# The last norm of a two-layer trunk: 1/rms of the last columns by logarithm and Exp, and one operation for weight and 1/rms

## The chip, the cores and the metric

The kernel runs on one core of a Trainium2 chip. Such a core has engines that run side by side, each with a queue of its own: TensorE (PE in the profile) multiplies matrices, VectorE (DVE) and ScalarE (ACT) work element by element, GpSimd (POOL) and SyncE (SP) here mostly issue transfers. An engine takes its queue in order and waits at an instruction until what it needs is there. Transfers between the chip's memory and the core's own memory (DMA) are issued from the queues of SP, ACT and POOL and run on 16 shared DMA engines. The metric is device time in microseconds, from the start of the program to its end; less is better.

## The reference

The reference is a decoder trunk for one sequence of 1024 positions with 1024 features: a short-convolution layer and a dilated-attention layer, each followed by a SwiGLU feed-forward block, and a norm at the very end. Only the end matters here:

```
def rms_norm(x, g):
    xf = x.astype(jnp.float32)
    y = xf * lax.rsqrt(jnp.mean(xf * xf, axis=-1, keepdims=True) + EPS)
    return (y * g.astype(jnp.float32)).astype(x.dtype)
...
        h = rms_norm(x, ffn_norm[i])
        x = x + swiglu(h, ffn_w_gate[i], ffn_w_up[i], ffn_w_down[i])
    return rms_norm(x, final_norm)
```

So every output element is x times 1/rms, which belongs to its position, times a weight (the gain), which belongs to its feature. The 1/rms of a position needs the squares of all its 1024 features, and these are complete only when the last product has been added to x.

## The kernel before

The residual x lies in eight tiles `X[n]`, n = 0 to 7, each of 128 partitions (features) and 1024 columns (positions). A gain is therefore one number per partition, and 1/rms is one number per column, the same in all partitions. A sum over features is a sum over partitions and over the eight tiles; TensorE makes it with a matrix of ones, which also puts the result into every partition.

A product in nearly full precision is made of three fast ones: each operand is split into a high part and a low remainder (`split`, lines 134 to 146: a copy on ScalarE at L144, a subtraction on VectorE at L145), and high by high, high by low and low by high are added up (lines 372 to 374). A product of two plain float32 operands is also possible; TensorE then runs it as two half-products.

The last feed-forward block ends with products that are done by columns (`by_columns`). The 1024 columns are cut into three pieces: 0 to 511, 512 to 767 and 768 to 1023. For each piece, and in it for each of the eight tiles n, TensorE makes twelve products (four tiles of the inner dimension, three parts each) into one of its eight accumulation banks; then `add_to_x` (L491, VectorE) adds the bank to x. In the first piece the weights are loaded and split as well, three tiles ahead. After each tile `each` and `between` (through `tile_done`), inside `final`, add their work to the queues:

- `each`: ScalarE squares the new columns of x (L1930 for tile 0, straight into the running sum `acc`; L1933 for the others, into a page `sq`). Then ScalarE multiplies the columns of x by the gain, in place (L1935).
- `between(i, n)`: VectorE adds the squares of the tile before to `acc` (`add_squares`, L1940), one tile behind so that it needn't wait for ScalarE. Then come the steps of the norm of the piece before, i - 1: at n = 1 its sum of squares is split (L144, L145); at n = 3 `spread_sums` multiplies both parts by ones (L485), and ScalarE makes 1/rms as Exp of -1/2 times the logarithm (L486, L487). At the same n = 3 the eight scalings of that piece are put into a list. Then one scaling is taken from the list (`some(1)`).
- `scaled`: one scaling, VectorE multiplies the columns of a tile by 1/rms (L1944), and the result is sent out (L1945), from SP's queue for even tiles and from ACT's queue for odd ones.

The order is written out by hand: each engine's queue holds its instructions in the order in which this code issues them. A scaling in `between` stands on VectorE ahead of the next tile's addition, and a transfer on ACT's queue stands ahead of the next square.

For the last piece there are no further tiles to do its norm beside, and it has a way of its own. `squared_sum` multiplies `acc` and the last tile's squares, 128 columns at a time, by one column of ones (L1958, L1960), which gives two columns with one sum per partition. ScalarE takes the square root, VectorE the reciprocal (L1963); VectorE makes from it and the identity matrix `eye` two diagonal matrices side by side (L1965), and `spread` multiplies these by ones (L1973), which brings 1/rms back into every partition. Between `squared_sum` and `spread` stand the scalings of the piece before that are left in the list. The root needs another function table on ScalarE than logarithm and Exp; it is loaded in piece 2 at n = 3 (L1990). The identity is loaded at the start, from POOL's queue (L1885).

Of the kernel before, what the change touches and what calls it, by code (L numbers as in the profile page):

```python
# [10 lines left out]
F32 = mybir.dt.float32  # L11
F32R = mybir.dt.float32r
AF = mybir.ActivationFunctionType
ALU = mybir.AluOpType
# [4 lines left out]
D = 1024  # L19
DF = 2816  # L20
H = 16
KT = D // 128
# [72 lines left out]
def view(t, off, dims):  # L95
    return bass.AP(tensor=t.tensor, offset=t.offset + off, ap=[t.ap[0]] + [list(d) for d in dims])
# [3 lines left out]
def trunk(ctx: ExitStack, tc: tile.TileContext, x, gains_in, cwi, ck, cwo, wqkv, wo, relb,  # L100
          wg, wu, wd, oneh, ident, out):
    nc = tc.nc
    consts = ctx.enter_context(tc.tile_pool(name="consts", bufs=1))
# [5 lines left out]
    def page(name, dt=F32):  # L109
        return pages.tile([128, 1024], dt, name=name, tag="page", bufs=PAGES)  # L110
# [3 lines left out]
    def half_page(name, dt=F32):  # L114
        return scope["pool"].tile([128, 512], dt, name=name, tag="half", bufs=scope["halves"])

    def bank():
        return psum.tile([128, 512], F32, name="bank", tag="bank")
# [7 lines left out]
    taps = consts.tile([128, KT, 3], F32)  # L126
    ones = consts.tile([128, 128], F32)
    ones_r = consts.tile([128, 128], F32R)
    eye = consts.tile([128, 128], F32)
    eps = consts.tile([128, 1], F32)  # L130
    scratch = consts.tile([128, 1], F32)
    zcol = consts.tile([128, 2, 1], F32)
# [32 lines left out]
    def ensure(upto):  # L165
        while op_state[0] < min(upto + 1, len(ops)):
            key = ops[op_state[0] + 1][0] if op_state[0] + 1 < len(ops) else None
            if key in sums_of:
                sums_of.pop(key)()
            made[op_state[0]] = ops[op_state[0]][1]()  # L170
            op_state[0] += 1

    def take(key, ahead=1):
        i = op_state[1]
        assert ops[i][0] == key, (ops[i][0], key)
        ensure(i + ahead)
        op_state[1] += 1
        return made.pop(i)
# [198 lines left out]
    def run(*gens):  # L377
        for _ in zip(*gens):
            pass
        for g in gens:  # L380
            for _ in g:
                pass
# [12 lines left out]
    X = [None] * KT  # L395
# [86 lines left out]
    def spread_sums(rstd, sums):  # L482
        b = bank()[:, :rstd.shape[1]]
        for i, t in enumerate(sums):
            nc.tensor.matmul(b, ones_r, t, start=i == 0, stop=i == len(sums) - 1)  # L485
        nc.scalar.activation(rstd, b, AF.Ln, scale=1.0 / D, bias=eps)  # L486
        nc.scalar.activation(rstd, rstd, AF.Exp, scale=-0.5)  # L487

    def add_to_x(n, banks):
        for (c0, c1), b in banks.items():  # L490
            nc.vector.tensor_tensor(out=X[n][:, c0:c1], in0=X[n][:, c0:c1], in1=b[:, :c1 - c0], op=ALU.add)  # L491
# [749 lines left out]
    class Swiglu(Strassen):  # L1241
# [111 lines left out]
        def feed_forward(self, stats, last_step, after, final=None):  # L1353
# [27 lines left out]
            if final:  # L1381
                final(key, self.plain, self.hid)
                return
# [4 lines left out]
    def by_columns(key, ks, acts, pieces, each, between, wide=4, ahead=1, added=lambda i, n: None):  # L1388

        w = {}  # L1390
        for i, piece in enumerate(pieces):
            for n in range(KT):
                if i == n == 0:
                    w.update({m: take(key + (m,)) for m in range(wide)})
                    ensure(op_state[1] + ahead)
                    banks = {m: {piece: bank()} for m in range(wide)}
                    run(*[product(w[m], ks, acts, banks[m]) for m in banks])
                elif i or n >= wide:
                    if i == 0:
                        w[n] = take(key + (n,), min(ahead, KT - 1 - n) or 1)  # L1400
                    banks = {n: {piece: bank()}}
                    run(product(w[n], ks, acts, banks[n]))
                add_to_x(n, banks[n])
                added(i, n)
                each(n, piece)
                between(i, n)
# [475 lines left out]

    load_first()
    nc.gpsimd.dma_start(taps, ck)
    nc.gpsimd.dma_start(eye, ident)  # L1885
    nc.vector.memset(ones, 1.0)
    nc.vector.memset(ones_r.bitcast(F32), 1.0)
    nc.vector.memset(eps, EPS)
# [6 lines left out]
    with tc.tile_pool(name="first", bufs=1) as scope["pool"]:  # L1895
# [4 lines left out]
        norm = Norm(1)  # L1900
# [13 lines left out]
    with tc.tile_pool(name="third", bufs=1) as scope["pool"]:  # L1914
        scope["halves"] = 20
        sw, group1, *rest = into_ffn(1, Norm(3))
        group1("ao", range(AO, 8), acts)
        norm = Norm(4)

        def final(key, ks, hid):  # L1920
            pieces = ((0, HALF), (HALF, 768), (768, S))
            sums, scale = [], []

            def each(n, c):

                s = slice(*c)
                if norm.acc is None:
                    norm.acc, norm.rstd = page("acc"), page("rstd")
                if n == 0:
                    nc.scalar.activation(norm.acc[:, s], X[n][:, s], AF.Square)  # L1930
                else:
                    sq = page("sq")
                    nc.scalar.activation(sq[:, s], X[n][:, s], AF.Square)  # L1933
                    sums.append((sq, s))
                nc.scalar.activation(X[n][:, s], X[n][:, s], AF.Identity, scale=norm.gain(n))  # L1935

            def add_squares(keep=0):
                while len(sums) > keep:
                    sq, s = sums.pop(0)
                    nc.vector.tensor_tensor(out=norm.acc[:, s], in0=norm.acc[:, s], in1=sq[:, s], op=ALU.add)  # L1940

            def scaled(i, n, rstd):
                s = slice(*pieces[i])
                nc.vector.tensor_tensor(out=X[n][:, s], in0=X[n][:, s], in1=rstd, op=ALU.mult)  # L1944
                (nc.sync, nc.scalar)[n % 2].dma_start(out[n][:, s], X[n][:, s])  # L1945

            def some(k):
                for _ in range(min(k, len(scale))):
                    scaled(*scale.pop(0))

            def squared_sum(i, extra=None):

                c0, c1 = pieces[i]
                nt = (c1 - c0) // 128
                b = bank()
                for t in range(nt):
                    cols = slice(c0 + 128 * t, c0 + 128 * t + 128)
                    nc.tensor.matmul(b[:, t:t + 1], norm.acc[:, cols], ones[:, 0:1], start=True, stop=extra is None)  # L1958
                    if extra is not None:
                        nc.tensor.matmul(b[:, t:t + 1], extra[:, cols], ones[:, 0:1], start=False, stop=True)  # L1960
                r = consts.tile([128, KT], F32, name="r", tag="r", bufs=2)
                nc.scalar.activation(r[:, :nt], b[:, :nt], AF.Sqrt, scale=1.0 / D, bias=eps)
                nc.vector.reciprocal(r[:, :nt], r[:, :nt])  # L1963
                diag = half_page("diag")
                nc.vector.tensor_tensor(out=view(diag, 0, [[128, nt], [1, 128]]),  # L1965
                                        in0=view(eye, 0, [[0, nt], [1, 128]]),
                                        in1=view(r, 0, [[1, nt], [0, 128]]), op=ALU.mult)
                return diag[:, :c1 - c0]

            def spread(diag):  # L1970
                b = bank()
                w = diag.shape[1]
                nc.tensor.matmul(b[:, :w], ones, diag, start=True, stop=True)  # L1973
                return b[:, :w]

            known = []

            def between(i, n):
                add_squares(int(n > 0))
                if (i, n) == (0, 5):  # L1980
                    nc.scalar.preload_act_table_set(LN_EXP)
                if i and n == 1:
                    s = slice(*pieces[i - 1])
                    known.append(split(norm.acc[:, s], [half_page("sum", F32R)[:, :s.stop - s.start] for _ in range(2)]))
                elif i and n == 3:
                    s = slice(*pieces[i - 1])
                    spread_sums(norm.rstd[:, s], known.pop())
                    scale.extend((i - 1, k, norm.rstd[:, s]) for k in range(KT))
                    if i == len(pieces) - 1:
                        nc.scalar.preload_act_table(AF.Sqrt)  # L1990
                some(1)

            def tile_done(i, n):
                if i < len(pieces) - 1 or n < KT - 1:
                    between(i, n)

            by_columns(key, ks, hid, pieces, each, tile_done, 1, 3)
            last = len(pieces) - 1
            add_squares(1)
            diag = squared_sum(last, sums.pop()[0])  # L2000
            some(KT)
            rstd = spread(diag)
            for n in range(KT):
                scaled(last, n, rstd)

        sw.feed_forward(*rest, None, final)


# [48 lines left out]
```

## Time and profile before

| what | value |
|---|---|
| median of three runs | 2113.32 us (2112.34 to 2113.49) |
| profiled execution | 2113.6 us |
| its span in the trace | 2111.8 us |
| TensorE busy | 2088.2 us, 99% of the span |
| VectorE busy | 1737.2 us, 82% |
| ScalarE busy | 1021.1 us, 48% |
| last product of the last block ends | 2100.1 us |
| last scaling ends | 2108.3 us |

The profile is one execution, recorded by the chip; its times are counted from the start of the span. In a row of the timeline stand the start, the duration, the engine, the line of the kernel, the operation, what is written from what, the shape, the count, and in brackets how long the engine had been idle and what ended that. A row with a count above one merges neighbours: its duration runs from the start of the first to the end of the last. Two instructions of one engine can overlap by a little, so the distance between two starts is often less than a duration. The rows of the windows give for a stretch of time its length, then the busy time of TensorE, of its weight loads, of VectorE, ScalarE and GpSimd, then the clock granted to TensorE (1.00 is full speed), the mean busy share of the DMA engines and the GB/s that they moved. The rows of groups give the busy time of all instructions of a kind and the mean in ns of one.

### The profile page before, as it was taken

To read this page: it belongs to the slowest core of one execution; us is meant where nothing else is said; L and a number is where in the kernel's file an instruction comes from. 1 tells how busy PE (TensorE), PEld (TensorE's weight loads), DVE (VectorE), ACT (ScalarE), POOL (GpSimd) and SP (SyncE) were. 2 spreads that over 40 slices of the span, in tenths; PEclk is the share of its full clock that TensorE was granted. 3 is DMA by queue.
4 is the path that set the end of the run, shared out by engine and by line. 5 is a ranking of instruction groups with operands and counts; after the bars stand their busy time and mean duration, and the time that the engine had idled before them with its cause. 6 is when DMAs were issued, how large, how long until landed. Compare 5 with 4: busy or idle time off the path is not lost. (4 is left out here: it accounts for less than half of the span.)

```text
span 2111.8 us, 30764 instructions
## 1 busy us (share of the span) xinstructions
PE 2088.2 (99%) x11006; PEld 1796.4 (85%) x11006; DVE 1737.2 (82%) x3255; ACT 1021.1 (48%) x1868; POOL 236.8 (11%) x337
## 2 busy tenths in 40 slices
PE   9999999999999999999999999999999999999998
PEld 7788888888888888887799999988788888888887
DVE  8898769988888888968967687987998888888876
ACT  7433427443434554446545555555544434456435
POOL 1000000110101000010322222211011011001000
PEclk9999999999999999999999999999999999999999
DMA  7322643323333476351767777955223333358432
GB/s 221 95 95 70 229 135 75 105 100 110 115 100 107 155 206 203 121 157 65 244 210 190 170 184 191 250 190 140 70 90 105 105 106 105 115 187 244 158 95 80
DMA packets 141527, 300.77 MB, mean 142 GB/s; under 512 B 48252, under 2 KB 54478, under 8 KB 141376
## 3 DMA queue, kind: packets, MB, share of 16 engines
q1 hardware_dynamic: 107488, 201.94, 32.7%
q0 software_dynamic: 26256, 82.18, 12.3%
q10 hardware_dynamic: 7632, 14.70, 1.8%
q8 instruction: 87, 1.43, 0.3%
q14 instruction: 64, 0.52, 0.1%
HBM read 208.49 MB, written 82.93 MB: 138 GB/s over the span
## 5 line engine op out<-in xcount | busy, mean ns | idle before, releaser
L572 PE MATMUL bank<-b,w 128*128 128x512 f32 x1952 | 761.3, 390 | 5.1 <-DVE w L145 4.9
L570 PE MATMUL bank<-b,w 128*128 128x512 f32 x1952 | 761.7, 390 | 3.6 <-ACT w L144 2.3
L571 PE MATMUL bank<-b,w 128*128 128x512 f32 x1952 | 761.2, 390 | 0.6 <-DVE b L881 0.6
L572 PEld LDWEIGHTS bank<-b,w 128*128 128x128 f32 x1952 | 366.9, 188 | 85.6 <-DVE w L145 9.4
L570 PEld LDWEIGHTS bank<-b,w 128*128 128x128 f32 x1952 | 367.0, 188 | 80.1 <-ACT w L144 3.1
L571 PEld LDWEIGHTS bank<-b,w 128*128 128x128 f32 x1952 | 367.1, 188 | 75.6 <-DVE b L881 1.5
L144 ACT ACTIVATE w<-combo 128x512 fp32r<-128x512 f32 (+2 forms) x488 | 249.2, 540 | 237.8 <-DVE combo L192 220.6
L145 DVE TENSOR_TENSOR w<-combo,w 128x512 fp32r<-128x512 f32 (+2 forms) x488 | 276.5, 580 | 37.9 <-ACT w L144 37.1
L576 ACT ACTIVATE part<-bank 128x512 f32<-128x512 f32 x186 | 110.7, 595 | 377.7 <-PE bank L572 377.4
L145 DVE TENSOR_TENSOR w<-raw,w 128x512 fp32r<-128x512 f32 (+2 forms) x342 | 189.8, 576 | 36.3 <-ACT w L144 36.3
L580 DVE TENSOR_TENSOR part<-part,bank 128x256 f32<-128x256 f32 (+1 forms) x366 | 170.7, 496 | 29.5 <-PE bank L572 16.7
L144 ACT ACTIVATE w<-raw 128x512 fp32r<-128x512 f32 (+2 forms) x342 | 166.8, 530 | 45.4 <-PE bank L572 11.5
L372 PE MATMUL bank<-w_hi,w 128*128 128x512 f32 (+1 forms) x400 | 150.8, 377 | 0.1
L374 PE MATMUL bank<-w_hi,w 128*128 128x512 f32 (+1 forms) x400 | 149.3, 373 | 0.7 <-DVE w L145 0.7
L373 PE MATMUL bank<-w_lo,w 128*128 128x512 f32 (+1 forms) x400 | 149.0, 372 | 0.0
L491 DVE TENSOR_TENSOR x<-x,bank 128x512 f32<-128x512 f32 (+1 forms) x104 | 66.2, 642 | 61.2 <-PE bank L374 60.8
L800 DVE TENSOR_TENSOR x<-x,bank 128x512 f32<-128x512 f32 x136 | 92.6, 681 | 28.8 <-PE bank L572 28.8
L192 DVE TENSOR_TENSOR combo<-raw 128x512 f32<-128x512 f32 (+1 forms) x172 | 111.1, 647 | 0.0
L374 PEld LDWEIGHTS bank<-w_hi,w 128*128 128x128 f32 x400 | 75.3, 188 | 14.8 <-DVE w L145 1.6
L563 DVE TENSOR_TENSOR b<-hin,b 128x512 fp32r<-128x512 f32 x126 | 79.4, 684 | 9.4 <-ACT b L562 9.4
L372 PEld LDWEIGHTS bank<-w_hi,w 128*128 128x128 f32 x400 | 75.5, 189 | 12.6 <-ACT w L144 0.5
L373 PEld LDWEIGHTS bank<-w_lo,w 128*128 128x128 f32 x400 | 75.5, 189 | 12.1
(241 smaller groups left out, 3452.8 us busy)
## 6 DMA issues: line engine op xcount, KB each, us to landing
hin<-part SPq DMA_DIRECT2D x126, 256.0 KB
raw<-in_ffn_w_gate SPq DMA_DIRECT2D x44, 512.0 KB
raw<-in_ffn_w_up SPq DMA_DIRECT2D x44, 512.0 KB
part<-sum POOLq DMA_DIRECT2D x72, 256.0 KB, 2.3
raw<-in_ffn_w_down SPq DMA_DIRECT2D x48, 384.0 KB
raw<-in_attn_w_qkv SPq DMA_DIRECT2D x27, 512.0 KB
raw<-in_conv_w_in SPq DMA_DIRECT2D x24, 512.0 KB
part<-part POOLq DMA_DIRECT2D x36, 256.0 KB, 2.6
```

Source lines behind the costliest of these rows:

```text
L144: nc.scalar.activation(hi, src, AF.Copy)
L145: eng.tensor_tensor(out=lo, in0=src, in1=hi, op=ALU.subtract)
L192: eng.tensor_tensor(out=c, in0=a, in1=b, op=op)
L372: nc.tensor.matmul(b, whi[:, a], ahi[:, s], start=first, stop=False)
L373: nc.tensor.matmul(b, whi[:, a], alo[:, s], start=False, stop=False)
L374: nc.tensor.matmul(b, wlo[:, a], ahi[:, s], start=False, stop=last)
L570: nc.tensor.matmul(b, hi[:, a], bhi, start=start and k == 0, stop=False, skip_group_check=True)
L571: nc.tensor.matmul(b, hi[:, a], blo, start=False, stop=False, skip_group_check=True)
L572: nc.tensor.matmul(b, lo[:, a], bhi, start=False, stop=k == n - 1, skip_group_check=True)
L576: nc.scalar.activation(t, b, AF.Copy)
L580: nc.vector.tensor_tensor(out=t, in0=t, in1=b, op=ALU.add)
L800: nc.vector.tensor_tensor(out=X[n][:, half(h)], in0=X[n][:, half(h)], in1=b, op=ALU.add)
```

## The change

The last piece gets its 1/rms in the way of the others, but with full-precision products: what is in `acc` and the squares of the last two tiles (which are no longer added up on VectorE) are multiplied by the 128 x 128 ones and added up in one bank, and ScalarE makes the logarithm and Exp of 256 columns. Root, reciprocal, diagonal, the table load for the root, `squared_sum`, `spread`, the tile `eye` and its load go.

ScalarE no longer multiplies x by the gain. `scaled` does both in one operation on VectorE: 1/rms times the gain of the partition times x.

The scalings are issued elsewhere: at n = 3 one scaling is taken from the list before the new ones are put in, so that in piece 1 none is issued there (the list is empty); in the last piece none is issued at n = 6 and n = 7. Those left over, six of piece 1 instead of four, are issued behind the last piece's logarithm and Exp.

```
-    eye = consts.tile([128, 128], F32)
...
-    nc.gpsimd.dma_start(eye, ident)
...
-                nc.scalar.activation(X[n][:, s], X[n][:, s], AF.Identity, scale=norm.gain(n))
...
             def scaled(i, n, rstd):
                 s = slice(*pieces[i])
-                nc.vector.tensor_tensor(out=X[n][:, s], in0=X[n][:, s], in1=rstd, op=ALU.mult)
+                nc.vector.scalar_tensor_tensor(X[n][:, s], rstd, norm.gain(n), X[n][:, s], op0=ALU.mult, op1=ALU.mult)
                 (nc.sync, nc.scalar)[n % 2].dma_start(out[n][:, s], X[n][:, s])
...
-            def squared_sum(i, extra=None):
...
-            def spread(diag):
...
             def between(i, n):
-                add_squares(int(n > 0))
+                last = i == len(pieces) - 1
+                if not (last and n == KT - 1):
+                    add_squares(int(n > 0))
                 if (i, n) == (0, 5):
                     nc.scalar.preload_act_table_set(LN_EXP)
...
                 elif i and n == 3:
                     s = slice(*pieces[i - 1])
                     spread_sums(norm.rstd[:, s], known.pop())
+                    some(1)
                     scale.extend((i - 1, k, norm.rstd[:, s]) for k in range(KT))
-                    if i == len(pieces) - 1:
-                        nc.scalar.preload_act_table(AF.Sqrt)
-                some(1)
-
-            def tile_done(i, n):
-                if i < len(pieces) - 1 or n < KT - 1:
-                    between(i, n)
-
-            by_columns(key, ks, hid, pieces, each, tile_done, 1, 3)
-            last = len(pieces) - 1
-            add_squares(1)
-            diag = squared_sum(last, sums.pop()[0])
+                    return
+                if not last or n < 6:
+                    some(1)
+
+            by_columns(key, ks, hid, pieces, each, between, 1, 3)
+            s = slice(*pieces[-1])
+            rstd = norm.rstd[:, s]
+            squares = [norm.acc[:, s]] + [sq[:, s] for sq, _ in sums]
+            b = bank()[:, :s.stop - s.start]
+            for i, t in enumerate(squares):
+                nc.tensor.matmul(b, ones, t, start=i == 0, stop=i == len(squares) - 1)
+            nc.scalar.activation(rstd, b, AF.Ln, scale=1.0 / D, bias=eps)
+            nc.scalar.activation(rstd, rstd, AF.Exp, scale=-0.5)
             some(KT)
-            rstd = spread(diag)
             for n in range(KT):
-                scaled(last, n, rstd)
+                scaled(len(pieces) - 1, n, rstd)
```

More of the change, by code (lines that the diff above doesn't have):

```diff
@@ L1949, in some @@
                     scaled(*scale.pop(0))
-            def squared_sum(i, extra=None):
[L1953 to L1968, printed above, removed]
-            def spread(diag):
[L1971 to L1974, printed above, removed]
             known = []
             def between(i, n):
-                add_squares(int(n > 0))
+                last = i == len(pieces) - 1
+                if not (last and n == KT - 1):
+                    add_squares(int(n > 0))
                 if (i, n) == (0, 5):
```

## The prediction

> **What bounds the kernel now.** I read the page first. Its busy shares say that TensorE sets the time of the whole run, so a change in the last stage is worth only what it takes off the end behind the last matrix product.
>
> ```profile
> span 2111.8 us, 30764 instructions
> PE 2088.2 (99%) x11006; PEld 1796.4 (85%) x11006; DVE 1737.2 (82%) x3255; ACT 1021.1 (48%) x1868; POOL 236.8 (11%) x337
> ```
>
> Next I read the timeline of TensorE over the last stage. The last residual products are done in three pieces of columns (512, 256, 256), eight tiles each; I write (p,n) for tile n of piece p, pieces 0 to 2. The first row below begins (1,4).
>
> ```profile
> 2081.77 0.28 PE L372 MATMUL bank<-w_hi,w 128*128 128x256 f32 x1
> ...
> 2093.15 0.28 PE L374 MATMUL bank<-w_hi,w 128*128 128x256 f32 x1
> 2093.50 0.84 PE L485 MATMUL bank<-sum,ones_r 128*128 128x256 f32 x2
> 2094.18 0.28 PE L372 MATMUL bank<-w_hi,w 128*128 128x256 f32 x1
> ...
> 2099.82 0.28 PE L374 MATMUL bank<-w_hi,w 128*128 128x256 f32 x1
> ...
> 2104.26 1.22 PE L1973 MATMUL bank<-diag,ones 128*128 128x256 f32 x2 [1.01 <-DVE diag L1965]
> ```
>
> From 2094.18 to 2099.82 stand four tiles of 12 products, 47 steps in 5.64: 0.12 a step, 1.44 a tile. The last product ends at 2100.10. Between 2093.15 and 2094.18 lie 1.03, of which 0.12 is the last product's own step and 0.24 the two sum products of L485; 0.67 is a stall. Then VectorE's timeline, which carries the end:
>
> ```profile
> 2084.73 0.69 DVE L1944 TENSOR_TENSOR x<-x,rstd 128x512 f32<-128x512 f32 x1 [2.11 <-ACT rstd L487]
> 2085.34 0.41 DVE L491 TENSOR_TENSOR x<-x,bank 128x256 f32<-128x256 f32 x1
> ...
> 2091.69 0.41 DVE L491 TENSOR_TENSOR x<-x,bank 128x256 f32<-128x256 f32 x1
> 2093.48 0.43 DVE L145 TENSOR_TENSOR sum<-acc,sum 128x256 fp32r<-128x256 f32 x1 [1.39 <-ACT sum L144]
> ...
> 2101.40 0.41 DVE L491 TENSOR_TENSOR x<-x,bank 128x256 f32<-128x256 f32 x1
> 2101.73 0.42 DVE L1940 TENSOR_TENSOR acc<-acc,sq 128x256 f32<-128x256 f32 x1
> 2103.58 0.17 DVE L1963 RECIPROCAL r<-r 128x2 f32<-128x2 f32 x1 [1.44 <-ACT r L1962]
> 2103.78 0.42 DVE L1965 TENSOR_TENSOR diag<-eye,r 128x256 f32<-128x256 f32 x1
> 2104.13 1.42 DVE L1944 TENSOR_TENSOR x<-x,rstd 128x256 f32<-128x256 f32 x4
> 2105.52 2.74 DVE L1944 TENSOR_TENSOR x<-x,bank 128x256 f32<-128x256 f32 x8
> ```
>
> The reader is to see that the last addition to x (2101.40) comes 1.30 after its product (2100.10): VectorE is late. Its lateness began at 2084.73, where (1,3) waited 2.11 for the 1/rms of piece 0 with the next addition queued behind. The product of (1,4) began at 2081.77 and was done 1.44 + 0.16 later (the last step's 0.28 less 0.12), at 2083.37, but was added at 2085.34. A tile then costs VectorE 0.33 (2101.40 to 2101.73) for the addition, as much for the sum of squares and 0.61 (2084.73 to 2085.34) for a scaling, below TensorE's 1.44, so the lag shrinks slowly and is renewed by the wait of 1.39 at 2093.48. Behind the last addition the end is a chain: sums, root, reciprocal, diagonal, four scalings of piece 1 left over, spread, eight scalings of piece 2, until 2108.26. The windows of the end show the transfers:
>
> ```profile
> 2103.00:2103.50 0.50, 0.25 (x3) 0.17 (x2) 0.00 (x0) 0.21 (x1) 0.00 (x0) 0.89 0.00 0
> ...
> 2105.00:2105.50 0.50, 0.48 (x2) 0.00 (x0) 0.50 (x2) 0.00 (x0) 0.00 (x0) 0.50 0.14 51
> 2105.50:2106.00 0.50, 0.00 (x0) 0.00 (x0) 0.50 (x3) 0.00 (x0) 0.00 (x0) 0.50 1.00 336
> ...
> 2110.00:2110.50 0.50, 0.00 (x0) 0.00 (x0) 0.00 (x0) 0.00 (x0) 0.00 (x0) 0.50 0.12 37
> ```
>
> The last three numbers are granted clock, share of the DMA engines, GB/s. The clock falls in the first of these rows, 2.9 to 3.4 after the last residual product. Twelve stores of 128 KB run without a gap from 2105.43 (0.14 of a half-microsecond) to 2110.06: 0.386 each. The first of them left a scaling that ended at 2104.55, so 0.88 lies between a scaling and its data. The span ends 1.74 after the last data.
>
> **The change part by part.** ScalarE's rows for it:
>
> ```profile
> 2092.18 0.42 ACT L1933 ACTIVATE sq<-x 128x256 f32<-128x256 f32 x1 [0.36 <-DVE x L491]
> 2092.63 0.51 ACT L1935 ACTIVATE x<-x,gains 128x256 f32<-128x256 f32 x1
> 2093.04 0.40 ACT L144 ACTIVATE sum<-acc 128x256 fp32r<-128x256 f32 x1
> ...
> 2097.05 0.46 ACT L486 ACTIVATE rstd<-bank,eps 128x256 f32<-128x256 f32 x1
> 2097.54 0.42 ACT L487 ACTIVATE rstd<-rstd 128x256 f32<-128x256 f32 x1
> 2097.97 1.28 ACT L1990 ACT_TABLE_LOAD   x1
> ...
> 2099.72 0.51 ACT L1935 ACTIVATE x<-x,gains 128x256 f32<-128x256 f32 x1
> 2099.78 0.34 ACTq L1945 DMA_DIRECT2D out<-x  x1
> ```
>
> *Weight taken from ScalarE (24 instructions at L1935) and put into the scaling.* On ScalarE each 256-wide one took a slot of about 0.41 (2092.63 to 2093.04); none is on the path except where ScalarE's next result is awaited, which is at the two splits. On VectorE a scaling becomes a three-operand operation with a weight per partition. The nearest rows:
>
> ```profile
> L1252 DVE SCALAR_TENSOR_TENSOR hcol<-x,gains,rstd 128x512 f32<-128x512 f32 x16 | 11.9, 746 | 3.4 <-ACT rstd L487 3.4
> L966 DVE SCALAR_TENSOR_TENSOR y<-part,taps,y 128x480 f32<-128x480 f32 x12 | 8.5, 711 | 0.0
> L966 DVE SCALAR_TENSOR_TENSOR y<-pad,taps,y 128x32 f32<-128x32 f32 x16 | 3.9, 245 | 0.0
> ```
>
> Between 480 and 32 columns lie 466 ns, 1.04 a column; 256 columns give 0.48, against 0.42 for the product of two. The four and eight rows of L1944 at the end start 0.33 apart (1.42 less 0.42, over 3) at a duration of 0.42, an overlap of 0.08, so I take a pace of 0.40 for 256 columns and 0.67 for 512. Bounds for the pace at 256: 0.34 (as now) and 0.67 (as for 512).
>
> *Order in (p,3).* The scaling that waited for the fresh 1/rms is no longer issued there; the wait of 2.11 goes, and piece 0's scalings begin in (1,4). There the 1/rms, at 2084.73 behind the gains of (1,2) and (1,3), comes two slots of 0.41 earlier, at 2083.9, and the scaling's turn is 2083.41 + 0.33 + 0.33 = 2084.07. A tile then costs VectorE 0.33 + 0.33 + 0.67 = 1.33, still below 1.44, so it stays with TensorE. The addition in (2,1) comes with its product too: that is done at 2090.57 (six tiles from 2081.77, and 0.16) and added at 2090.61 instead of 2091.69, its square follows, and the split's copy without a gain between: halves ready at 2092.4, ahead of the L485 products due at 2093.27. The 0.67 stall goes, and the last product ends at 2100.10 - 0.67 = 2099.43. What is late next is (2,3), by 0.85 (the split's subtraction and two scalings of 0.67 stand before it); by (2,7), with one scaling of 0.40 each in (2,4) and (2,5) and none in (2,6) and (2,7), it has caught up. So the last addition starts at 2099.47, 1.93 earlier. Bounds: 0 (lag as now) and 1.93.
>
> *Behind the last addition.* It ends at 2099.88 and the square at 2100.35. Three full-precision products of 256 columns replace eight one-column ones; two of them (the sum, the square of (2,6)) run while the square of (2,7) is made. The one product of this shape in the trace took 1.22 at a granted clock of 0.50. At full clock the nearest row is
>
> ```profile
> 1128.08 1.06 PE L1646 MATMUL bank<-lh,vx 128*128 128x128 f32 x8
> ```
>
> eight half-products of 128 columns in 1.06, some 0.11 each, so 0.22 for a half and 0.43 for a product of 256, plus some 0.2 until it can be read: 0.63. It starts at 2100.37, within 1 us of the last residual product, while the old profile kept full clock for 2.9 at least, so I take 0.63; sums at 2101.0. By the Trainium skill ("TensorE: Matmul & The Clock Gate", What's actually happening) the clock halves only after about 3.4 us without work, which gives the 0.63 and the sum below; were it at half here, the 1.22 would put the last data at 2107.1, since the stores nearly cover it. [...] Then the logarithm and Exp, 0.94 from start to VectorE's next (2097.05 to 2097.99): 1/rms at 2101.97. No table is loaded: the load at 2097.97 goes, and at (1,3) and (2,3) squares, logarithm and Exp follow each other with none. The reciprocal, the diagonal and the spread go.
>
> *Six scalings left over instead of four* ((0,0) not in (1,3), none in (2,6), and (2,7) had none already). They run on VectorE from 2099.81, six at 0.40, until 2102.21, which is 0.24 past the 1/rms. Cover is nearly enough; that 0.24 is the cost. Eight more at 0.40: the last starts at 2105.01 and ends at 2105.49, against 2108.26.
>
> *Stores.* Fourteen of 128 KB instead of twelve lie behind the last addition. SyncE's ((1,2), (1,4), (1,6)) go as they come: data from 2101.2, 2102.0, 2102.8. ScalarE's ((1,3), (1,5), (1,7)) are queued behind Exp, which starts at 2101.5; its queue issues while an activation runs (2099.78 above), 0.34 each: data from 2102.5. From then on the transfers are back to back, and twelve of them, 4.6, end at 2107.06. The last scaling alone would give 2105.49 + 0.88 + 0.39 = 2106.8; the stores bind by a little. The end is 2110.06 - 2107.06 = 3.0 earlier. With the pace of 0.34 the stores still bind at about 2106.5 (gain 3.5); with 0.67 the last scaling would end near 2109.3 and nothing would be gained.
>
> *The identity's load at the start* goes from POOL's queue; nothing waits behind it but the loads of the bias tables.
>
> ```profile
> eye<-in_identity POOLq DMA_DIRECT2D x1, 64.0 KB, 5.0
> ...
> 7.37 1.41 ACT L880 ACTIVATE b<-x,gains 128x512 fp32r<-128x512 f32 x2 [0.99 <-DMA x<-in_x]
> ```
>
> There ScalarE waits for x while the transfers are full; at the 0.386 per 128 KB of the end, 64 KB are 0.19. I take 0.15; bounds 0 and 0.19.
>
> The sum: 3.0 + 0.15, about 3.15, against the profiled execution's 2113.6 us (span 2111.8), so 2110.45. The median of the three runs, 2113.32, lies 0.28 below that execution: 2110.2.
>
> **The rivals.** *The lag stays.* If VectorE still meets the last addition at 2101.40 (three-operand scalings nearer 0.8 for 512 columns make a tile 1.46, over 1.44), everything behind moves by 1.93: gain 1.2, 2112.1. For it: the margin of 0.11 a tile. Against: (2,6) and (2,7) carry no scaling.
>
> *Faster by over 0.2% (4.2 us): the low clock near the start goes.*
>
> ```profile
> 28.00:29.00 1.00, 1.00 (x4) 0.78 (x3) 1.00 (x3) 1.00 (x3) 0.00 (x0) 0.54 0.00 0
> 29.00:30.00 1.00, 1.00 (x4) 0.81 (x3) 0.96 (x3) 1.00 (x2) 0.00 (x0) 0.50 0.00 0
> 30.00:31.00 1.00, 1.00 (x4) 0.71 (x4) 1.00 (x3) 1.00 (x3) 0.27 (x1) 0.50 0.00 0
> 31.00:32.00 1.00, 1.00 (x5) 0.81 (x4) 0.96 (x3) 1.00 (x2) 0.63 (x1) 0.75 0.00 0
> ```
>
> The missing clock adds to 0.46 + 0.50 + 0.50 + 0.25 = 1.71. With 3.15 that is 4.86: 2108.5. For it: the start moves by 0.15. Against: VectorE and ScalarE are at 0.95 to 1.00 throughout, so they set the idle time that is punished. The same section of the Trainium skill says that the window is free-running, so the phase may change by itself; no run shown tells.
>
> *Slower than before: the buffers move.* Without the identity everything allocated behind it starts 512 bytes lower in each partition. If that lengthened TensorE's steps, 3.15 in 2088.2, or 0.15%, would cancel the gain; at 0.35% the time is 2117.4. Against: pages rotate over many addresses already and the steps shown are 0.12 everywhere. For it: nothing in the trace.
>
> **How the numbers follow.** The forecast 0.72, the lag 0.14, the low clock 0.08, the moved buffers 0.06. The forecast's own range is 2109.2 to 2111.5, from the bounds of pace, stores and lag. With the lag and the spread of the runs it is 2108.9 to 2112.5, which leaves out the low clock and the moved buffers, 0.14. 0.2% is 4.2 us, about what a measurement of this kernel can tell from no change; 3.15 is 0.15%. Faster: the low clock and a little of the forecast's tail, 0.12; slower: most of the moved buffers, 0.05; the rest, 0.83, within.
>
> **What would show it.** In the changed profile: no wait for 1/rms in (1,3); TensorE's steps without the 0.67 hole before (2,4); the last addition some 0.04 after the last product; scalings of 256 columns at 0.48, 0.40 apart; three products of 256 columns at full clock; fourteen stores back to back, the last data near 2107. The prediction is wrong if VectorE is still late at the last addition, if a three-operand scaling takes over 0.6, or if a time moves outside the last 40 us.

## The result, and the profile after

The changed kernel takes 2109.41 us (median of 22 runs, 2108.25 to 2111.12), the kernel before, run beside it, 2112.86 us (22 runs, 2111.49 to 2115.91). The ratio is 0.9984, with a 95% interval of 0.9979 to 0.9990: 3.4 us less, between 2.1 and 4.4. The forecast was 3.15 less.

The profiled execution has a span of 2106.5 against 2111.8, which is 5.3 less and more than the medians say. To see what of it belongs to the change I need a mark that both traces share and behind which alone the change can act. The first addition of piece 1, (1,0), is such a mark. In the timeline of VectorE it stands here in the kernel before:

```profile
2077.18 0.42 DVE L491 TENSOR_TENSOR x<-x,bank 128x256 f32<-128x256 f32 x1
```

and in the changed kernel, with the rows that answer to those shown before, here:

```profile
2074.75 0.42 DVE L490 TENSOR_TENSOR x<-x,bank 128x256 f32<-128x256 f32 x1
...
2081.30 0.42 DVE L1937 TENSOR_TENSOR acc<-acc,sq 128x256 f32<-128x256 f32 x1
2081.63 0.74 DVE L1941 SCALAR_TENSOR_TENSOR x<-rstd,gains,x 128x512 f32<-128x512 f32 x1
...
2089.37 0.42 DVE L144 TENSOR_TENSOR sum<-acc,sum 128x256 fp32r<-128x256 f32 x1 [0.79 <-ACT sum L143]
...
2097.03 0.42 DVE L490 TENSOR_TENSOR x<-x,bank 128x256 f32<-128x256 f32 x1 [0.68 <-PE bank L373]
2097.37 5.62 DVE L1941 SCALAR_TENSOR_TENSOR x<-rstd,gains,x 128x256 f32<-128x256 f32 x14
```

So 2.43 of the 5.3 lie ahead of the mark. Of the change only the identity's load, the buffers that it moves and the missing gains of piece 0 can act there, and the gains don't reach the mark: from the first addition of piece 0 (2056.71 before, 2054.28 after) to the mark it is 20.47 in both. Behind the mark, the span is 34.62 before and 31.75 after: 2.87. Spans are given to 0.1, so these distances are good to some 0.05. The first scaling (2081.63) follows the sum of squares without a wait. The last addition is released by TensorE: VectorE idles 0.68 for it. The fourteen scalings that follow have no gap among them.

TensorE's timeline of the changed kernel at the two places of interest:

```profile
2090.72 0.28 PE L373 MATMUL bank<-w_hi,w 128*128 128x256 f32 x1
2090.83 0.40 PE L484 MATMUL bank<-sum,ones_r 128*128 128x256 f32 x2
2091.07 0.28 PE L371 MATMUL bank<-w_hi,w 128*128 128x256 f32 x1
...
2096.71 0.28 PE L373 MATMUL bank<-w_hi,w 128*128 128x256 f32 x1
2096.83 0.59 PE L1974 MATMUL bank<-acc,ones 128*128 128x256 f32 x2
2097.26 1.39 PE L1974 MATMUL bank<-sq,ones 128*128 128x256 f32 x4
```

From 2090.72 to 2091.07 it is 0.35, where it was 1.03: the hole is gone. The last product ends at 2096.99, and the last addition follows in 0.04 instead of 1.30. ScalarE's tail, and the windows in which the last transfers run (granted clock, DMA share and GB/s are the last three numbers):

```profile
2097.48 0.42 ACT L1931 ACTIVATE sq<-x 128x256 f32<-128x256 f32 x1 [1.02 <-DVE x L490]
2098.69 0.47 ACT L1975 ACTIVATE rstd<-bank,eps 128x256 f32<-128x256 f32 x1 [0.79 <-PE bank L1974]
2099.20 0.42 ACT L1976 ACTIVATE rstd<-rstd 128x256 f32<-128x256 f32 x1
2099.26 4.11 ACTq L1942 DMA_DIRECT2D out<-x  x7
```

```profile
2098.50:2099.00 0.50, 0.15 (x1) 0.00 (x0) 0.50 (x3) 0.31 (x1) 0.00 (x0) 1.00 0.56 190
...
2100.50:2101.00 0.50, 0.00 (x0) 0.00 (x0) 0.50 (x3) 0.00 (x0) 0.00 (x0) 1.00 1.03 332
...
2104.50:2105.00 0.50, 0.00 (x0) 0.00 (x0) 0.00 (x0) 0.00 (x0) 0.00 (x0) 0.50 0.53 176
```

The last data is there at about 2104.77, 1.73 before the span's end, as before.

Counted from the mark, in microseconds:

| | before | forecast | after |
|---|---|---|---|
| last product ends | 22.92 | 22.25 | 22.24 |
| last addition starts | 24.22 | 22.29 | 22.28 |
| last scaling ends | 31.08 | 28.31 | 28.24 |
| last data | 32.88 | 29.88 | 30.02 |
| end of the span | 34.62 | 31.62 | 31.75 |

The forecast's column is the prediction's times less 2077.18; its last number is the old span's end of 34.62 less the forecast gain of 3.0 at the end.

### The profile page after: what moved, and what is told of

Its sections match the earlier page's. It is cut to its first block, busy times and chain, and to the rows that moved or that the text cites. A ratio compares the mean times of both kernels' runs of the same rounds, so it can differ in the third digit from the quotient of the medians.

```text
span 2106.5 us, 30731 instructions
## 1 busy us (share of the span) xinstructions
PE 2084.7 (99%) x11002; PEld 1793.2 (85%) x11002; DVE 1738.8 (83%) x3252; ACT 1006.9 (48%) x1844; POOL 236.2 (11%) x336
```

## The experiments

All are read by the end of the span from the same mark. The changed kernel repeats there within 0.07 (31.75, 31.82 with nothing altered, 31.76 with the identity put back), while whole runs of one kernel spread over 2 to 4 us, so that the whole time tells differences of 0.5 us only poorly. For the kernels made from the one before, the interval of the ratio includes 1 each time; what is said of their gains rests on these distances, from one trace each. The marks and the ends that they come from:

| kernel | mark | end of the span | distance |
|---|---|---|---|
| changed again | 2076.18 | 2108.0 | 31.82 |
| changed, identity put back | 2076.74 | 2108.5 | 31.76 |
| before, logarithm and Exp | 2076.13 | 2109.2 | 33.07 |
| before, new order | 2076.20 | 2110.4 | 34.20 |
| before, one operation | 2076.07 | 2109.4 | 33.33 |
| changed, old order | 2076.49 | 2108.2 | 31.71 |
| changed, gain on ScalarE | 2076.48 | 2108.1 | 31.62 |
| before, new order and one operation | 2075.39 | 2109.1 | 33.71 |
| changed, without six stores | 2074.83 | 2106.0 | 31.17 |
| a little faster | 2077.26 | 2108.5 | 31.24 |

### The changed kernel again, and with the identity put back

> The changed kernel itself, as the mark for the three beside it. My theory: the gain of 2.9 us lies behind the last product and in the one hole before (2,4), and some 0.5 us at the start. Ratio to before 0.9983 to 0.9987, so 2.8 to 3.5 us. In its profile the distance from the first addition of piece 1 to the last data must again be about 30.0 us (2074.75 to 2104.75); before it was 32.9 (2077.18 to 2110.06). If the larger part came from the clock near the start, this distance would stay and the total would vary by up to 1.7 us from run to run with the clock.

It took 2109.69 us, ratio 0.9985 (0.9976 to 0.9994). The last data is 30.02 from the mark, as expected, and the span's end 31.82. The edit of the kernel beside it:

```
     taps = consts.tile([128, KT, 3], F32)
+    eye = consts.tile([128, 128], F32)
...
     nc.gpsimd.dma_start(taps, ck)
+    nc.gpsimd.dma_start(eye, ident)
```

> The changed kernel with the identity tile and its load put back, unused. My theory: 64 KB more among the first loads cost 0.2 to 0.6 us, and nothing changes at the end: 2.5 to 3.0 us faster than before. Rival (the load's removal shifts the start so that the low clock around 28 to 32 us goes): 1.7 us or more come back, and this kernel is only about 1.2 us faster than before. Rival (the moved buffers): the distance between TensorE's steps changes; I expect 0.12 as it was.

It took 2109.24 us, ratio 0.9983 (0.9974 to 0.9991): not slower than the changed kernel without the load, and 3.8 us faster than before. The expected 0.2 to 0.6 us isn't seen; the intervals are too wide to exclude it. The rival of 1.7 us isn't borne out: it would have put this kernel at about 2111.8. The last product ends 22.24 from the mark here too, so the moved buffers change no step of this stage.

A part of what moves the whole time is the low clock of TensorE. It comes in stretches of some 3.4 us, near 28 us and near 1161 us, in some executions and not in others. The windows of before, of the changed kernel and of the changed kernel again, in this order:

```profile
28.00:29.00 1.00, 1.00 (x4) 0.78 (x3) 1.00 (x3) 1.00 (x3) 0.00 (x0) 0.54 0.00 0
1161.00:1162.00 1.00, 0.83 (x4) 0.83 (x5) 1.00 (x3) 0.97 (x3) 0.00 (x0) 0.65 0.83 183
1162.00:1163.00 1.00, 1.00 (x7) 1.00 (x7) 0.97 (x3) 1.00 (x3) 0.00 (x0) 0.50 0.49 143
```

```profile
28.00:29.00 1.00, 1.00 (x6) 0.84 (x5) 0.96 (x3) 1.00 (x3) 0.00 (x0) 1.00 0.00 0
1161.00:1162.00 1.00, 0.67 (x7) 0.54 (x5) 0.98 (x3) 1.00 (x3) 0.00 (x0) 1.00 0.28 83
```

```profile
28.00:29.00 1.00, 1.00 (x6) 0.83 (x5) 1.00 (x3) 1.00 (x2) 0.00 (x0) 1.00 0.00 0
1161.00:1162.00 1.00, 0.91 (x4) 0.61 (x4) 1.00 (x3) 1.00 (x3) 0.00 (x0) 0.50 0.38 114
```

The third row of the first fence shows that the stretch goes on. The profiled execution of before has both stretches, that of the changed kernel has neither, the second one of the changed kernel has one. Of the kernels below, some with and some without the identity have the first: it doesn't follow the change. It doesn't explain all of the 2.43 ahead of the mark, though. The same operation of VectorE (it writes the tile `combo`) starts at 28.66 before and at 28.07 after: 0.59 are there as the first stretch begins. A later one of its kind starts at 62.11 and 60.55, an operation on the tile `m` at 1161.57 and 1160.05, and another behind the second stretch at 1179.65 and 1177.21. So 0.97 came between 28 and 62 us, in or behind the first stretch, and 0.92 with the second. The 0.59 isn't the change's either, as far as these traces tell: in the changed kernel again the operation near 28 us starts at 28.82, and with the identity put back at 28.11. Why the start differs stays open.

### Logarithm and Exp alone

```
-                    if i == len(pieces) - 1:
-                        nc.scalar.preload_act_table(AF.Sqrt)
...
-            last = len(pieces) - 1
-            add_squares(1)
-            diag = squared_sum(last, sums.pop()[0])
+            add_squares(2)
+            s = slice(*pieces[-1])
+            rstd = norm.rstd[:, s]
+            squares = [norm.acc[:, s]] + [sq[:, s] for sq, _ in sums]
+            b = bank()[:, :s.stop - s.start]
+            for i, t in enumerate(squares):
+                nc.tensor.matmul(b, ones, t, start=i == 0, stop=i == len(squares) - 1)
+            nc.scalar.activation(rstd, b, AF.Ln, scale=1.0 / D, bias=eps)
+            nc.scalar.activation(rstd, rstd, AF.Exp, scale=-0.5)
             some(KT)
-            rstd = spread(diag)
```

> The kernel before with only the last piece's 1/rms made as logarithm and Exp of squares times ones. My theory: the last addition stays 1.3 us behind its product; from it to the first scaling of piece 2 it takes 2.6 instead of 4.1 us; 1.4 to 1.8 us faster than before. With the new order alone this should add up to the changed kernel's 2.9 less the cost of the wider scaling. Rival (the stores bind from the first scaling on, so a shorter chain is worth nothing): under 0.4 us.

Measured: 2111.69 us, ratio 0.9994 (0.9986 to 1.0003). From the mark the span ends at 33.07, 1.55 less than before. VectorE's rows:

```profile
2096.95 0.43 DVE L1944 TENSOR_TENSOR x<-x,rstd 128x256 f32<-128x256 f32 x1 [1.55 <-ACT rstd L487]
...
2100.30 0.42 DVE L491 TENSOR_TENSOR x<-x,bank 128x256 f32<-128x256 f32 x1
2100.63 1.43 DVE L1944 TENSOR_TENSOR x<-x,rstd 128x256 f32<-128x256 f32 x4
2102.96 2.77 DVE L1944 TENSOR_TENSOR x<-x,rstd 128x256 f32<-128x256 f32 x8 [0.90 <-ACT rstd L2004]
```

From the last addition (2100.30) to the first scaling of piece 2 it is 2.66, and 4.12 before (2101.40 to 2105.52): as expected. The wait of 1.55 in (2,3) is still there, and the last addition is as late as before (24.17 from the mark).

### The order alone

```
                     spread_sums(norm.rstd[:, s], known.pop())
+                    some(1)
                     scale.extend((i - 1, k, norm.rstd[:, s]) for k in range(KT))
                     if i == len(pieces) - 1:
                         nc.scalar.preload_act_table(AF.Sqrt)
-                some(1)
+                    return
+                if i < len(pieces) - 1 or n < 6:
+                    some(1)
```

> The kernel before with only the new order of the scalings (none at n = 3 for the fresh 1/rms, none in (2,6)). My theory: no wait in (1,3), no hole before (2,4), the last addition right behind its product, 1.9 us sooner; but six scalings of 0.34 instead of four stand between diagonal and spread, and fourteen stores bind: 1.0 to 1.3 us faster than before. Rival (the lag of VectorE is hidden anyway): no faster than 0.3 us.

Measured: 2111.54 us, ratio 0.9994 (0.9985 to 1.0003). The span ends 34.20 behind the mark, 0.42 less than before and less of a gain than the 1.0 expected. The hole before (2,4) went (last product's end at 22.26), but the last addition is at 22.72, 0.46 behind. VectorE's rows and ScalarE's say why:

```profile
2097.58 0.43 DVE L1940 TENSOR_TENSOR acc<-acc,sq 128x256 f32<-128x256 f32 x1 [0.97 <-ACT sq L1933]
...
2101.55 0.42 DVE L1965 TENSOR_TENSOR diag<-eye,r 128x256 f32<-128x256 f32 x1
2101.89 2.10 DVE L1944 TENSOR_TENSOR x<-x,rstd 128x256 f32<-128x256 f32 x6
2103.90 2.73 DVE L1944 TENSOR_TENSOR x<-x,bank 128x256 f32<-128x256 f32 x8
```

```profile
2095.83 1.28 ACT L1991 ACT_TABLE_LOAD   x1
2097.13 0.42 ACT L1933 ACTIVATE sq<-x 128x256 f32<-128x256 f32 x1
```

The table load for the root keeps the square of (2,4) back, and VectorE waits 0.97 for it. In the kernel before that load hid behind VectorE's own lag; with the lag gone its cover is gone. Then six scalings stand where four stood: 2.10 instead of 1.42, on the path.

### Weight and 1/rms in one operation alone

```
-                nc.scalar.activation(X[n][:, s], X[n][:, s], AF.Identity, scale=norm.gain(n))
...
-                nc.vector.tensor_tensor(out=X[n][:, s], in0=X[n][:, s], in1=rstd, op=ALU.mult)
+                nc.vector.scalar_tensor_tensor(X[n][:, s], rstd, norm.gain(n), X[n][:, s], op0=ALU.mult, op1=ALU.mult)
```

> The kernel before with only weight and 1/rms in one operation, the scaling order and the root as they were. My theory: VectorE's tile grows to 1.34 to 1.43 against TensorE's 1.44, so its lag shrinks no more; the fresh 1/rms comes up to 0.8 sooner without the gains; twelve scalings at the end cost 0.06 more each, mostly under the stores: between 0.2 us faster and 0.7 us slower than before. Rival (the move from ScalarE is the gain): 1 us or more faster.

Measured: 2111.21 us, ratio 0.9993 (0.9984 to 1.0002); from the mark 33.33, 1.29 less than before. My theory fell here, and the rival held. VectorE's rows:

```profile
2082.54 0.75 DVE L1943 SCALAR_TENSOR_TENSOR x<-rstd,gains,x 128x512 f32<-128x512 f32 x1 [1.39 <-ACT rstd L487]
...
2095.22 0.48 DVE L1943 SCALAR_TENSOR_TENSOR x<-rstd,gains,x 128x256 f32<-128x256 f32 x1 [1.02 <-ACT rstd L487]
...
2098.80 0.42 DVE L491 TENSOR_TENSOR x<-x,bank 128x256 f32<-128x256 f32 x1
```

The waits for the fresh 1/rms remain, but they are shorter (1.39 for 2.11, 1.02 for 1.55), since ScalarE comes to logarithm and Exp sooner. The hole before (2,4) goes with this alone (last product's end at 22.24), and the last addition is at 22.73.

### The changed kernel with the old order

```
                     spread_sums(norm.rstd[:, s], known.pop())
-                    some(1)
                     scale.extend((i - 1, k, norm.rstd[:, s]) for k in range(KT))
-                    return
-                if not last or n < 6:
+                if not last or n < KT - 1:
                     some(1)
```

> The changed kernel with the scalings issued as before: the first scaling of a piece at n = 3, directly behind the order for its 1/rms, and one in (2,6). My theory: VectorE waits about 1 us for Exp in (1,3) and again in (2,3), its tile then costs 1.43 against TensorE's 1.44, so the lag stays; the last addition is 1.5 to 2.2 us behind its product and the whole about 1.5 us slower than the changed kernel (1.9 us faster than before). Rival (the order is of no matter, VectorE is served sooner because ScalarE has no gains): within 0.3 us of the changed kernel.

Measured: 2110.00 us, ratio 0.9983 (0.9974 to 0.9991); from the mark 31.71, against 31.75. My theory fell, and the rival held: the order is worth nothing here. VectorE's rows:

```profile
2082.96 0.75 DVE L1941 SCALAR_TENSOR_TENSOR x<-rstd,gains,x 128x512 f32<-128x512 f32 x1 [1.39 <-ACT rstd L486]
...
2099.22 0.42 DVE L490 TENSOR_TENSOR x<-x,bank 128x256 f32<-128x256 f32 x1
2099.55 1.67 DVE L1941 SCALAR_TENSOR_TENSOR x<-rstd,gains,x 128x256 f32<-128x256 f32 x4
2101.88 3.25 DVE L1941 SCALAR_TENSOR_TENSOR x<-rstd,gains,x 128x256 f32<-128x256 f32 x8 [0.66 <-ACT rstd L1974]
```

The last addition is 0.45 later than in the changed kernel, not 1.5: its distance from the mark is 22.73. From (2,4) on a tile costs VectorE 1.07 (2098.15 to 2099.22 for the last), 0.37 under TensorE's 1.44, and the lag melts. And the 0.45 buys something: only four scalings are left over, twelve stores follow instead of fourteen, and the last data is at 29.97, where the changed kernel has 30.02.

### The changed kernel with the gain back on ScalarE

The edit is that of the one operation, backwards.

> The changed kernel with the gain back on ScalarE and scalings of two operands. My theory: the copy of the split in (2,1) comes 0.45 later and is still 0.5 ahead of the products that need it, so no hole returns before (2,4); scalings are 0.34 apart, the last ends 0.6 sooner, and the stores bind: 0.1 to 0.4 us faster than the changed kernel. Rival (taking the gain from ScalarE is what lets the split be in time): the hole of 0.4 or more returns and it is 0.3 us or more slower.

Measured: 2109.54 us, ratio 0.9985 (0.9976 to 0.9994); from the mark 31.62, 0.13 less than the changed kernel, as expected, though little more than the 0.07 by which the changed kernel itself differs. VectorE's rows:

```profile
2098.77 0.42 DVE L490 TENSOR_TENSOR x<-x,bank 128x256 f32<-128x256 f32 x1 [0.55 <-PE bank L373]
...
2101.38 2.77 DVE L1942 TENSOR_TENSOR x<-x,rstd 128x256 f32<-128x256 f32 x8 [0.18 <-ACT rstd L1977]
```

The last addition is at 22.29, released by TensorE, so with the order new, the move of the gain isn't needed either.

### All but logarithm and Exp

The kernel before with both edits, the order and the one operation.

> The kernel before with the new order and the one operation, but the old root and diagonal for the last piece: all but logarithm and Exp. From the first addition of piece 1 to the end of the span it was 34.62 before, 34.20 with the order alone, 33.33 with the one operation alone. If the two do the same thing for VectorE, the last addition is at 22.28 behind that mark (as in the changed kernel), but six scalings of 0.40 stand between diagonal and spread and fourteen stores follow: 33.5 to 33.9, worse than the one operation alone. Rival (the two add up): 32.9 or less.

Measured: 2112.89 us, ratio 1.0001 (0.9991 to 1.0011); from the mark 33.71, worse than the one operation alone, inside what was expected. VectorE's rows:

```profile
2097.68 0.42 DVE L491 TENSOR_TENSOR x<-x,bank 128x256 f32<-128x256 f32 x1 [0.28 <-PE bank L374]
...
2100.42 2.46 DVE L1943 SCALAR_TENSOR_TENSOR x<-rstd,gains,x 128x256 f32<-128x256 f32 x6
2102.79 3.22 DVE L1943 SCALAR_TENSOR_TENSOR x<-bank,gains,x 128x256 f32<-128x256 f32 x8
```

VectorE has no lag at all, and the table load delays nothing here, where ScalarE has no gains. And yet the six wider scalings, behind a diagonal that they needn't wait for but stand behind in the queue, take 2.46 on the path. So the three edits, by the end of the span from the mark:

| order | weight | root | log and Exp |
|---|---|---|---|
| old | on ScalarE | 34.62 | 33.07 |
| new | on ScalarE | 34.20 | 31.62 |
| old | in the scaling | 33.33 | 31.71 |
| new | in the scaling | 33.71 | 31.75 |

### Without six stores

```
-                (nc.sync, nc.scalar)[n % 2].dma_start(out[n][:, s], X[n][:, s])
+                if i != 1 or n < 2:
+                    (nc.sync, nc.scalar)[n % 2].dma_start(out[n][:, s], X[n][:, s])
```

> The changed kernel without the stores of the six scalings left over (tiles 2 to 7 of piece 1 are not written out, so that part of the output is missing). If the stores bind at the end, as I summed it, the last data comes 0.88 + 0.39 behind the last scaling, at 29.5 behind the first addition of piece 1 instead of 30.03, and the span is about 0.5 us shorter from that mark (31.2 instead of 31.75). If the chain of operations sets the end, nothing changes.

Measured from the mark, in a single run: 31.17, 0.58 less than the changed kernel; the last scaling ends at 28.25 in both. The last data is at 2104.39, which is 29.56 from this trace's mark at 2074.83:

```profile
2104.00:2104.50 0.50, 0.00 (x0) 0.00 (x0) 0.00 (x0) 0.00 (x0) 0.00 (x0) 0.50 0.77 254
```

So the stores do bind the end of the changed kernel, by 0.5.

### A version that is a little faster

```
+                nc.scalar.activation(X[n][:, s], X[n][:, s], AF.Identity, scale=norm.gain(n))
...
-                nc.vector.scalar_tensor_tensor(X[n][:, s], rstd, norm.gain(n), X[n][:, s], op0=ALU.mult, op1=ALU.mult)
-                (nc.sync, nc.scalar)[n % 2].dma_start(out[n][:, s], X[n][:, s])
+                nc.vector.tensor_tensor(out=X[n][:, s], in0=X[n][:, s], in1=rstd, op=ALU.mult)
+                queue = nc.sync if i < len(pieces) - 1 else (nc.sync, nc.scalar)[n % 2]
+                queue.dma_start(out[n][:, s], X[n][:, s])
...
-                if not last or n < 6:
+                if not last or n < 7:
```

> The changed kernel with the gain on ScalarE, scalings of two operands, one scaling put back into (2,6), where VectorE idles 0.3 us, and the stores of the first two pieces all from SyncE's queue, so that none waits behind Exp. My theory: five scalings are left over and end before the 1/rms; the last scaling ends 0.6 sooner, thirteen stores start 0.7 sooner on average: 0.5 to 1.0 us faster than the changed kernel, 3.9 to 4.4 us faster than before. If the stores do not bind it gains only 0.6; if the scaling in (2,6) delays the last addition, less than 0.3.

Measured: 2108.32 us, ratio 0.9980 (0.9971 to 0.9989), 4.2 us by the ratio; from the mark 31.24, 0.51 less than the changed kernel, the lower end of what was expected. Its windows show what it ran into:

```profile
2103.50:2104.00 0.50, 0.00 (x0) 0.00 (x0) 0.50 (x3) 0.00 (x0) 0.00 (x0) 0.50 0.82 264
2104.50:2105.00 0.50, 0.00 (x0) 0.00 (x0) 0.43 (x2) 0.00 (x0) 0.00 (x0) 0.50 1.03 336
...
2106.50:2107.00 0.50, 0.00 (x0) 0.00 (x0) 0.00 (x0) 0.00 (x0) 0.00 (x0) 0.50 0.50 166
```

While the stores of the leftover scalings come from one queue only, 264 GB/s are moved, 128 KB in 0.50; with two queues it is 336. So a backlog forms. The last scaling ends at 27.67 from the mark, which alone would put the last data at 28.94 (0.88 and 0.39 behind it); it is at 29.49. That the slower single queue is what cost the rest of the hoped-for gain is my reading of these rows; no run sets it apart.

## Why the prediction was right

*The size and the place.* Forecast 3.15 with a range that ends at 0.8 and 4.4 below; measured 3.4 by the medians and 2.87 by the end of the traces, where 3.0 was forecast. The change stayed within 0.2%, the outcome that had been given 0.83. That the medians come so near 3.15 is in part luck: the interval of the ratio, 2.1 to 4.4, doesn't tell 3.15 from 2.9.

*The hole of 0.67 and the last addition* came out as summed: 22.24 and 22.28 against 22.25 and 22.29. *The chain behind it*: 2.71 from the last addition to the first scaling of piece 2, as worked out from the pace of the scalings, were forecast to be 2.74 (the six scalings stand in between and end it), and fourteen scalings in 5.62 are 0.395 apart ((5.62 less 0.48) over 13) where 0.40 was taken. *The products at full clock*: from the end of the last square to the logarithm it took 0.79, where 0.68 was summed; the clock was 1.00 there, and by half the clock's price it would have been 1.2 and more. The rule that the prediction cites for it, that the clock halves only after about 3.4 us without work, isn't what these traces show. Before, the clock fell at 2103.39, when TensorE had been at the small sums from 2102.20 to 2103.25; that the fall came 2.9 to 3.4 behind the last residual product is no sign of that much idleness. The last section has more on it. *The stores*: they bind, as the kernel without six of them shows; the last data is at 30.02, 0.14 later than summed.

*The step that failed, though it cost no number*, is "Order in (p,3)". It gave the 1.93 of the last addition to the order of the scalings. The table shows that each of two edits does it alone, the new order or the gain's leaving ScalarE: with logarithm and Exp in place, either one brings 1.4 (33.07 to 31.62 or 31.71), and both together bring no more than one. The prediction priced the gain's slot on ScalarE only at the splits and the fresh 1/rms's 0.8, and did not ask whether that alone would close the hole; it does, with a last addition that is 0.45 behind that of the new order (22.73 against 22.28, logarithm and Exp in place). Since the change makes both edits, the sum came out all the same.

*The table load*, which the prediction let go at no gain, is worth something: with the new order and the root, VectorE waits 0.97 for a square behind it. So logarithm and Exp bring 1.55 where VectorE lags anyway (34.62 to 33.07), and 2.58 with the new order (34.20 to 31.62). Of these 1.03 more, 0.43 are the load's absence (last addition at 22.29 instead of 22.72). By my reading the rest is the six scalings, which stand on the path behind the diagonal and run beside the chain behind logarithm and Exp.

*The rivals.* The lag didn't stay. The moved buffers changed no step of the last stage. The low clock did go in the profiled execution, but it comes and goes without the change. The rival's price of 1.71 for the first stretch was too simple as well: the kernel before with logarithm and Exp alone has that stretch, and the operation that starts at 28.78 there, 0.71 behind the changed kernel, is followed by one at 60.86, only 0.31 behind. The prediction didn't see the second stretch. *The identity's load* was priced at 0.15; no run shows that term: its removal can't be told from nothing here. The 0.5 between the medians' 3.4 and the end's 2.87 stays open: it lies inside the interval of the ratio.

## What to carry to other kernels

When two edits free the same engine, the sum of their prices counts the gain twice or gives it to the wrong one; ask of each wait whether shortening it or moving it away from the queue would each do alone. Work left over at the end should stand beside the last chain and not inside it: six scalings cost 2.1 to 2.5 us behind a diagonal and nearly nothing beside logarithm and Exp. And where whole runs spread by several microseconds, a mark that both traces share, just ahead of the change, reads it to a tenth.

## What the runs showed of the hardware

The low clock of TensorE came in stretches of 3.41 us at the same two places of the program in some executions and not in others (one trace has one near 8 us instead), with one core at work and TensorE busy 99% of the span. At half clock, each can cost TensorE at most half of its length. In the seven traces that have the second stretch, the operation of VectorE behind it comes 0.9 to 1.2 us later, counted from the one ahead of it, than in the changed kernel's first trace, which doesn't have it; in the other four it comes within 0.03. This goes into the spread of 2 to 4 us between runs: of the changed kernel's 22 runs, the five with a mean granted clock of 0.997 take 2110.1 us on average, the twelve with 0.998 2109.6, the five with 0.999 2108.6.

The changes of the clock lie on a grid. In the trace of before they are at 28.08, 31.50, 1161.31, 1164.72 and 2103.39, which is 1, 331, 1 and 275 times 3.413 apart. TensorE wasn't idle in the 3.41 ahead of the three falls, as the windows of before show (its busy time is the second number):

```profile
24.67:28.08 3.41, 1.82 (x7) 1.21 (x8) 3.32 (x7) 3.41 (x6) 0.00 (x0) 1.00 0.01 4
1157.89:1161.31 3.42, 1.85 (x14) 1.44 (x13) 3.39 (x10) 3.32 (x7) 0.00 (x0) 1.00 1.03 275
2099.97:2103.39 3.42, 1.18 (x10) 0.97 (x8) 2.17 (x7) 2.90 (x8) 0.00 (x0) 1.00 0.33 115
```

In the changed kernel's first trace the grid lies otherwise against the work, and at the same two places the clock stays:

```profile
24.77:28.18 3.41, 2.51 (x10) 1.78 (x11) 3.41 (x7) 3.41 (x6) 0.00 (x0) 1.00 0.01 2
1157.99:1161.41 3.42, 2.22 (x14) 1.80 (x14) 3.35 (x9) 3.35 (x7) 0.00 (x0) 1.00 0.87 206
```

So in these traces it is enough that TensorE is busy for about half of such a stretch or less, and where the grid falls decides whether a gap is met. The limit isn't sharp here: over the twelve traces no fall follows a stretch with more than 0.63, and some stretches with 0.50 to 0.63 are followed by one and some are not.

Stores of 128 KB from SyncE's queue alone moved 264 GB/s, from two queues 332 to 344. A table load of 1.28 us was followed by the next activation after 0.02 us (2095.83 and 2097.13).
